# A tenth projection unit in seven products, thinner filler and an earlier softmax scaling in a neighbourhood attention layer

## The chip, the core and the metric

The kernel runs on one core of one Trainium2 chip. The metric is the device time of one execution in microseconds. The core's engines are TensorE (PE in the profile, PEld its weight loads), VectorE (DVE), ScalarE (ACT), GpSimd (POOL) and SyncE (SP), which here issues nearly all DMAs. Each runs its own instructions in the order of the program and waits for the others by semaphores.

## What is computed

One layer (DEPTH is 1) on 2048 tokens of width 1024, in float32, 16 heads of 64; the tokens form a grid of 32 rows of 64.

```
h = rmsnorm(x, norm_0)
q, k, v, gate = split(h @ w_in_0, 4)          # 1024 -> 4 x 1024
s = q . k / 8 + rpb                           # keys: 8 rows x 16 columns around the query
o = softmax(s) . v
x = x + (o * silu(gate)) @ w_out_0
out = rmsnorm(x, norm_f)
```

## The kernel before

Every product of the projections is made of three TensorE products in a faster 32-bit format: the operands are split into a high and a low part (ScalarE copies the high part, VectorE subtracts it), and high x high, high x low and low x high are summed.

Stage one and stage two make the projections of the first and of the second half of the tokens. A unit is 256 columns of q, k or gate (four units each, j = 0 to 3). "By seven" is Strassen's way: seven products of half the size on sums of the operands, 7 x 12 = 84 TensorE products of 128x512 for a unit and a token half, where the plain way takes 96. Stage two does nine units by seven (`units_two`); the last unit of q, k and gate (j = 3) is left for the attention loop, as `halves`: one entry is a unit on one quarter of the tokens, two `group`s of 24 products. `items` are the loads and splits that those need: weights ("w"), the last four blocks of x ("x", normalised on VectorE, split on ScalarE, remainder on VectorE) and the output weights ("o"). `consume` splits one item.

The attention loop (`for m in range(cycles + 1)`) runs over 32 cycles, one for each pair of heads and quarter of the tokens. This text calls round m the piece that begins with the transposes of cycle m - 1:

- `turns(m - 1)`: 44 transposes (`ph`) of the softmax weights; six copies to SBUF (`pta`), three on ScalarE (L1347), three on VectorE (L1345);
- `scores(2m)`, `scores(2m + 1)`: two runs of scores (`s`), each with four minima and sums on VectorE (L1306) and four exponentials on ScalarE (L1312);
- `values(m - 1)`: the product with v (`o`), its gating on VectorE (`og`, L1380) and its store (`ogd`);
- then, from the head of cycle m + 1, filler: products of `halves` (L392, L394, L396), later of the output projection (L1580, L1582, L1584). `feed(n)` issues about n of them; `amount` is the table of products for each cycle. Among them stands `normalise(2m + 1)`, the second run's softmax scaling: one reciprocal (L1317) and two products on VectorE (L1322), one on ScalarE (L1324), one on POOL (L1326). `consume` and `split_rows` stand there too.

What ends a group follows its last product: `give` for q, k and gate (gate: ScalarE's tanh L372, VectorE's `sg` L373), `add_rows` for output rows (`y`, L1452, later a Square, L1455). A clock counts the filler products, and `store` puts an action at a count: `load_q` and `load_k` of the next cycle stand at the counts 7 and 12 of a cycle, the store of `og` at 4 after `values`. What of the loads has not come by the end of a cycle is issued by `all_loads` at the next one's head. The first scaling, `normalise(2m)`, is issued within the second run of scores.

After the loop the last 12 of 16 row tiles of the output projection, six pairs, are made by seven as well (`rows_by_seven`).

Of the kernel before, what the change touches and what calls it, by code (L numbers as in the profile page):

```python
# [77 lines left out]
def build(ctx, tc, x, xr, xt, wg, bias, w_out, n0, nf, out):  # L78
# [178 lines left out]
    def units(k, j):  # L257
        return [KINDS[k] + j + i for i in range(2 if k == "v" else 1)]

    units_two = [(k, j) for j in range(3) for k in "kqg"]  # L260
    halves = [(k, 3, 1, c) for g in ("k", "qg") for c in (2, 3) for k in g]
    attending = [False]
    last_use = {}
    for n, (k, j, ph, c) in enumerate(halves):
# [5 lines left out]
    for n, (k, j, ph, c) in enumerate(halves):  # L270
        a = (KINDS[k] + j, ph)
# [36 lines left out]
    def consume(n, asked=False, turn=False):  # L308
        for _ in range(n):
            load_ahead()  # L310
            if attending[0] and not asked and not turn:
                return
            if state["used"] == len(items) or not may_use(items[state["used"]]):
                return
            if attending[0] and now() - asked_at[items[state["used"]]] < 36 and not asked:
                return
            it = items[state["used"]]
            state["used"] += 1
            use_item(it)
# [18 lines left out]
    def store(key, lag, f):  # L338
        n = len(later)
        while n and later[n - 1][0] > clock[0] + lag:  # L340
            n -= 1
        later.insert(n, (clock[0] + lag, key, f))

    def due(n):
        clock[0] += n
        while later and later[0][0] <= clock[0]:
            later.pop(0)[2]()
# [848 lines left out]
    def projections():  # L1196
        for n, (kind, j, ph, c) in enumerate(halves):
            state["half"] = n
            w = (KINDS[kind] + j, ph)
            for a in range(2):  # L1200
                if n == len(halves) - 5 and a == 0:
                    for k in range(RES_EARLY):
                        load_res(*turns_[k])
                if n == len(halves) - 1:
                    if a == 0:
                        load_og(0)
                        load_og(1)
                    else:
                        store(("og0",), 9, lambda: split_og(0))
                consume(1)  # L1210
                p = yield from group(w, a, c, n)
                state["event"] = clock[0]
                give(kind, 2 * j + a, c, p, True)
            state["done_halves"] = n + 1
# [191 lines left out]
    def load_og(n):  # L1406
        T, i = divmod(n, 4)
        must(*[("og", p, T) for p in range(NP)])
        G[n] = t = wp([128, NK, 128], F32, "ograw")
        nc.sync.dma_start(t, ogd[T][:, i])  # L1410

    def load_res(n, j):
        RES[n, j] = rbp([128, 512], F32, "xr")
        nc.sync.dma_start(RES[n, j], x[n * 128:n * 128 + 128, 512 * j:512 * j + 512])

    def split_og(n):
        t = G[n]
        state["event"] = clock[0]
        h, l = wp([128, NK, 128], F32R, "gh"), wp([128, NK, 128], F32R, "gl")
        for j in range(2):  # L1420
            s = slice(4 * j, 4 * j + 4)
            nc.scalar.activation(h[:, s], t[:, s], AF.Copy)
            nc.vector.tensor_tensor(l[:, s], t[:, s], h[:, s].bitcast(F32), OP.subtract)
        G[n] = [(h[:, i], l[:, i]) for i in range(NK)]
# [93 lines left out]
    def run_scales():  # L1518
        while rooted:
            n, scale, send = rooted.pop(0)  # L1520
            scale()
            store(("y", n), 18, send)
# [12 lines left out]
    def split_rows():  # L1535
        n = ready["split"]
        if rows_due():
            split_og(n)
            ready["split"] += 1
            return True  # L1540
# [201 lines left out]
                        f(*a)  # L1742

    cycles = len(order)
    dense, end_of_it = 13.5, 24
    amount = [dense] * 25
    first = 16
    amount[0] -= first / 2
# [1 line left out]
    for m in range(8, 24):  # L1750
        amount[m] += 1.5 if m % 2 == 0 else -1.5
    calm_debt = 3
    amount += [(96 * (12 - len(units_two)) + 48 * PLAIN - sum(amount) - first - end_of_it) / (cycles - 25)] * (cycles - 25) + [end_of_it]
    fill = projections()
    outs = outputs()
    credit = [0.0]
    alive = [True]

    def feed(n, calm=0):
        credit[0] += n  # L1760
        while credit[0] > 0 or credit[0] > -calm_debt and clock[0] - state["event"] < calm:
            if alive[0]:
                got = next(fill, None)
                if got is None:
                    alive[0] = False
                    continue
            else:
                got = next(outs, None)
                if got is None:
                    due(max(credit[0], 0.0))  # L1770
                    credit[0] = min(credit[0], 0.0)
                    return
            credit[0] -= got
            due(got)
# [30 lines left out]
    for m in range(cycles + 1):  # L1805
        a = amount[m] - 8
        begin(m)
        feed(8)
        if m:
            due_here = []  # L1810
            quiet[0] = True
            if a < 12 and m > 8 and m % 2:
                normalise(2 * m - 1, True, lambda: due_here.append(split_rows() or consume(1, turn=True)))
            else:
                normalise(2 * m - 1, True)
            most, behind = 99 if a > 12 else 0 if rows_due() else 1, bool(rooted)
            run_scales()
            if not (behind or any(due_here)):
                run_roots(most)
            for k in range(3):  # L1820
                if m == 1 and k == 2:
                    pass
                elif a > 12 or not any(due_here) and (k < 1 or k < 2 and m > 8 and m % 2 == 0):
                    got = split_rows()
                    due_here.append(got)
                    if not got:
                        consume(1, turn=True)
                    elif a < 12 and m % 2 == 0 and len(items) - state["used"] == 8:
                        feed(a * 0.2)
                        consume(1, turn=True)  # L1830
                feed(a * 0.2)
        else:
            feed(a * 0.6)
        quiet[0] = False
        feed(a * 0.4, 8 if a > 12 else 4)
        if m:
            turns(m - 1)
        if m == cycles:
            all_loads()
            feed(6)  # L1840
            while next(outs, 0) != 0:
                due(1)
            land_T2()
            for n in range(3):
                form_rows(n, 1)
        else:
            scores(2 * m)
            if m == 0:
                feed(first)
            scores(2 * m + 1, lambda: normalise(2 * m))  # L1850
            if m == 0:
                consume(2, turn=True)
        if m:
            values(m - 1)
        runs[0] += 1
        if m == 8:
            late_loads()
# [37 lines left out]
```

## Time and profile before

| | |
|---|---|
| median of 3 runs | 997.88 us (997.6 to 998.34) |
| profiled execution | 998.06 us, its span 996.0 us |
| TensorE busy | 986.9 us, 99% of the span, 6892 matmul records |
| VectorE, ScalarE, POOL busy | 772.9, 541.6, 128.5 us |
| granted TensorE clock | 0.999 |
| HBM | 160.31 MB read, 66.06 MB written, 227 GB/s |

The attention loop's first transposes begin at 575.3 us, its last at 871.4. A row of the timeline or of the chain begins with its start and its length in us, then the engine; `x44` counts the instructions that a row merges; what stands in brackets is idle time ahead of it and who ended it. A matmul's own length overlaps with the next one's, so the pace of TensorE is read from start to start. The rows that the prediction rests on stand there.

### The profile page before, as it was taken

The numbers are of one execution on the slowest core, as the hardware profiler recorded it, in microseconds if no ns is written. First come the engines' busy times: TensorE is split into PE (matmuls) and PEld (weight loads), VectorE is DVE, ScalarE is ACT, GpSimd is POOL, SyncE is SP. The second block draws the span as 40 slices with busy tenths as digits, with TensorE's granted clock in tenths as the row PEclk, the third lists the DMA queues.
The fourth block names the chain that finished last, engine by engine and source line by source line (L and its number), as shares of the span: only waits on it lengthen the run. The fifth ranks groups of instructions, "written<-read, shape, count | busy, mean of one in ns | idle before, by whom it ended". The sixth has DMA issues, their size and how long they took to land.

```text
span 996.0 us, 19496 instructions
## 1 busy us (share of the span) xinstructions
PE 986.9 (99%) x6892; PEld 789.4 (79%) x6892; DVE 772.9 (78%) x1703; ACT 541.6 (54%) x1310; POOL 128.5 (13%) x204
## 2 busy tenths in 40 slices
PE   9999999999999999999999999999999999999997
PEld 6888888888888888888888777777776777788886
DVE  5899888987665876766776687788889888886866
ACT  7863245465535442333433377777777786653443
POOL 0000001231100000000000022223232322201110
PEclk9999999999999999999999999999999999999999
DMA  8933547777947846656565798888978787997754
GB/s 285 347 116 104 195 134 255 246 250 251 363 150 222 275 123 194 205 174 213 175 191 195 229 286 270 271 240 261 320 231 290 244 251 236 329 358 199 196 153 116
DMA packets 150120, 227.65 MB, mean 229 GB/s; under 512 B 13640, under 2 KB 65096, under 8 KB 150024
## 3 DMA queue, kind: packets, MB, share of 16 engines
q1 hardware_dynamic: 147000, 221.30, 69.1%
q0 software_dynamic: 2592, 4.72, 2.9%
q8 instruction: 54, 0.88, 0.4%
q10 hardware_dynamic: 432, 0.40, 0.1%
q14 instruction: 42, 0.34, 0.1%
HBM read 160.31 MB, written 66.06 MB: 227 GB/s over the span
## 4 chain that ended last, share of the span: by engine, by line
PE 97%; ACT 1%; DVE 1%; DMA 0%; SPq 0%; issue 0%; POOL 0%; DVEq 0%; POOLq 0%
PE pp L448 40%; PE pv L614 13%; PE py L1674 11%; PE o L1376 8%; PE s L1297 7%; PE ph L1357 4%; PE pp L394 3%; PE pp L396 2%; PE pp L392 2%; PE pv L729 2%; PE po L1582 1%; PE po L1584 1%; PE po L1580 1%; DMA land<-in_xt_dram 0%; ACT x L1312 0%; DVE pta L1345 0%
## 5 line engine op out<-in xcount | busy, mean ns | idle before, releaser
L448 PE MATMUL pp<-h,f 128*128 128x512 f32 x576 | 185.4, 389 | 0.0
L448 PE MATMUL pp<-t,f 128*128 128x512 f32 x702 | 171.3, 389 | 0.0
L448 PEld LDWEIGHTS pp<-t,f 128*128 128x128 f32 x702 | 131.8, 188 | 27.4
L1326 POOL TENSOR_SCALAR x<-x,st 128x360 f32<-128x360 f32 (+5 forms) x160 | 81.8, 527 | 526.2 <-DVE st L1317 526.2
L1312 ACT ACTIVATE x<-x,st 128x360 f32<-128x360 f32 (+5 forms) x256 | 134.2, 526 | 26.9 <-DVE st L1306 26.8
L448 PEld LDWEIGHTS pp<-h,f 128*128 128x128 f32 x576 | 108.1, 188 | 22.5
L448 PE MATMUL pp<-l,f 128*128 128x512 f32 x288 | 112.1, 389 | 0.0
L1306 DVE CUSTOM_DVE_ANT_0 x<-s,em 128x360 f32<-128x360 f32 (+5 forms) x256 | 102.7, 457 | 2.2 <-issue 0.7
L431 DVE TENSOR_TENSOR f<-raw,f 128x512 fp32r<-128x512 f32 x105 | 75.8, 726 | 19.9 <-ACT f L430 19.7
L1376 PEld LDWEIGHTS o<-pta,vt 120*64 120x64 f32 (+2 forms) x1024 | 68.7, 137 | 22.4 <-DVE st L1306 15.2
L430 ACT ACTIVATE f<-raw 128x512 fp32r<-128x512 f32 x105 | 63.6, 622 | 37.1 <-DVE raw L437 22.0
L1376 PE MATMUL o<-pta,vt 120*64 120x192 f32 (+5 forms) x1024 | 83.5, 316 | 0.0
L1297 PE MATMUL s<-kt,q 64*64 64x360 f32 (+5 forms) x1024 | 73.1, 413 | 0.4 <-DVE pta L1345 0.3
L1347 ACT ACTIVATE pta<-ph 120x512 f32<-120x512 f32 (+5 forms) x96 | 48.9, 556 | 33.8 <-PE ph L1357 33.7
L1345 DVE COPY pta<-ph 120x512 f32<-120x512 f32 (+5 forms) x96 | 56.0, 638 | 13.4 <-PE ph L1357 13.1
L448 PEld LDWEIGHTS pp<-l,f 128*128 128x128 f32 x288 | 54.0, 188 | 11.3
L1674 PE MATMUL py<-woh,f 128*128 128x512 f32 x192 | 60.9, 390 | 0.0
L614 PE MATMUL pv<-wh,t 128*128 128x512 f32 x176 | 56.2, 389 | 0.0
L1297 PEld LDWEIGHTS s<-kt,q 64*64 64x64 f32 x1024 | 36.5, 132 | 21.7 <-DVE pta L1345 4.9
L448 PE MATMUL pp<-sixths,f 128*128 128x512 f32 x198 | 52.7, 389 | 0.0
L1357 PEld LDWEIGHTS ph<-ident,x 64*120 64x120 f32 (+2 forms) x1408 | 42.6, 128 | 11.7 <-issue 10.6
L430 ACT ACTIVATE f<-s 128x512 fp32r<-128x512 f32 x42 | 26.2, 624 | 45.6 <-DVE s L437 40.4
(227 smaller groups left out, 1872.8 us busy)
## 6 DMA issues: line engine op xcount, KB each, us to landing
raw<-in_wg_dram SPq DMA_DIRECT2D x124, 256.0 KB, 5.1
row<-in_xr_dram SPq DMA_DIRECT2D x32, 256.0 KB, 5.4
vd<-v SPq DMA_DIRECT2D x32, 256.0 KB, 5.0
sgd<-sg SPq DMA_DIRECT2D x32, 256.0 KB, 3.2
q<-qd SPq DMA_DIRECT2D x32, 256.0 KB, 5.8
sgt<-sgd SPq DMA_DIRECT2D x32, 256.0 KB, 7.0
ogd<-og SPq DMA_DIRECT2D x32, 256.0 KB, 3.4
kt<-kd SPq DMA_DIRECT2D x16, 480.0 KB, 6.4
```

The costliest lines, as they stand in the source:

```text
L430: nc.scalar.activation(t[:, 0], src, AF.Copy)
L431: nc.vector.tensor_tensor(t[:, 1], src, t[:, 0].bitcast(F32), OP.subtract)
L448: nc.tensor.matmul(B[n, P], t[:, int(m == 2), c], x[k][int(m == 1)], start=P in (1, 6, 5) and k == 0 and m == 0, stop=k == 3 and m == 2, s ...
L614: nc.tensor.matmul(p, a[:, o], b, start=P in (1, 6, 5) and k == 0 and m == 0, stop=k == 3 and m == 2, skip_group_check=True)
L1297: nc.tensor.matmul(places[C, s][h * 64:h * 64 + 64], qt[a, g * 64:g * 64 + 64], kt[a, :r1 - r0, c0:c0 + 8 * WIDE[C]].rearrange("p r (s c) ...
L1306: nc.vector.tensor_tensor_reduce(X[i, C][s], pst[s], EM[p, ROW_TYPE[T]][C > 0][s], -1.0, 1e38, OP.add, OP.min, st[:, o:o + 1])
L1312: nc.scalar.activation(X[i, C][s], X[i, C][s], AF.Exp, bias=st[:, o:o + 1], scale=-1.0, accum_out=st[:, 4 + o:5 + o])
L1326: nc.gpsimd.tensor_scalar(X[i, C][s], X[i, C][s], st[:, o:o + 1], 1.0, op0=OP.mult, op1=OP.mult)
L1345: nc.vector.tensor_copy(o, i_)
L1357: nc.tensor.transpose(ph[b, h][:k, o:o + 64], X[2 * m + late_, group[g]][s][q, at:at + k], ident[q, q])
L1376: nc.tensor.matmul(o[s * 64:s * 64 + 64, g0 * 64:g1 * 64], vt[:k, strip, s * 64:s * 64 + 64], t[:k, n * 64:(n + g1 - g0) * 64], start=stri ...
L1674: nc.tensor.matmul(B[m, P], t[:, a, c], b, start=P in (1, 6, 5) and k == 0 and i == 0, stop=k == 3 and i == 2, skip_group_check=True)
```

## The change

The k unit j = 3 joins `units_two`, so stage two does ten units by seven and the loop is left with q and gate of j = 3, in four halves. `dense`, the base of `amount` for the first 25 cycles, goes from 13.5 to 10.8; the later ones take what is left. The head of a cycle issues 5 (`HEAD`) instead of 8 filler products before `normalise`, and the other 3 after the first split. The hooks that load residual rows, the first rows of the output projection and split them are set to the halves that are left, and that split comes at the count 14 instead of 9.

```
-    units_two = [(k, j) for j in range(3) for k in "kqg"]
-    halves = [(k, 3, 1, c) for g in ("k", "qg") for c in (2, 3) for k in g]
+    units_two = [(k, j) for j in range(3) for k in "kqg"] + [("k", 3)]
+    halves = [(k, 3, 1, c) for c in (2, 3) for k in "qg"]
...
-                if n == len(halves) - 5 and a == 0:
+                if n == 0 and a == 1:
                     for k in range(RES_EARLY):
                         load_res(*turns_[k])
                 if n == len(halves) - 1:
-                    if a == 0:
+                    if a == 1:
                         load_og(0)
                         load_og(1)
-                    else:
-                        store(("og0",), 9, lambda: split_og(0))
+                        store(("og0",), 14, lambda: split_og(0))
...
-    dense, end_of_it = 13.5, 24
+    dense, end_of_it = 10.8, 24
...
+    HEAD = 5
...
-        feed(8)
+        feed(HEAD)
...
-                feed(a * 0.2)
+                feed(a * 0.2 + (8 - HEAD if k == 0 else 0))
         else:
-            feed(a * 0.6)
+            feed(a * 0.6 + 8 - HEAD)
```

Counted in the order of TensorE's instructions, the filler products of rounds 1 to 31 were 11 14 13 14 13 14 15 | 12 15 12 15 12 15 15 12 12 15 12 15 12 18 9 15 | 12 13 14 13 14 13 17 20, and are 11 11 11 10 11 11 13 | 9 15 6 12 10 12 9 13 10 12 12 9 9 12 10 11 | 9 12 7 9 10 9 13 20 (the bars stand behind rounds 7 and 23). In the changed kernel the line numbers of the places below are one lower.

VectorE in round 0, from behind the minima and sums to the copies of round 1, before (`raw` and `l` are a block of x, its normalised form and its low part; `w` a weight's low part; `x` the softmax weights, `pta` their transposes):

```order
L542 SCALAR_TENSOR_TENSOR raw<-raw,g_174,rb 128x512
L547 TENSOR_TENSOR l<-raw,h 128x512
L542 SCALAR_TENSOR_TENSOR raw<-raw,g_174,rb 128x512
L547 TENSOR_TENSOR l<-raw,h 128x512
L1317 RECIPROCAL st<-st 128x4
L1322 TENSOR_SCALAR x_5286<-x_5286,st 128x264
L1322 TENSOR_SCALAR x_5287<-x_5287,st 128x264
L194 TENSOR_TENSOR w<-raw,w 128x512 x2
L1345 COPY pta<-ph_5374 88x6x64
```

And in the changed kernel, at the same place:

```order
L194 TENSOR_TENSOR w<-raw,w 128x512 x2
L1316 RECIPROCAL st<-st 128x4
L1321 TENSOR_SCALAR x_5423<-x_5423,st 128x264
L1321 TENSOR_SCALAR x_5424<-x_5424,st 128x264
L542 SCALAR_TENSOR_TENSOR raw<-raw,g_174,rb 128x512
L547 TENSOR_TENSOR l<-raw,h 128x512
L542 SCALAR_TENSOR_TENSOR raw<-raw,g_174,rb 128x512
L547 TENSOR_TENSOR l<-raw,h 128x512
L1344 COPY pta<-ph_5503 88x6x64
```

The two blocks of x have changed places with the two weights, and stand between the scaling and the copies; two more blocks, not shown, stand at the same place in rounds 1 and 2, where one weight stood.

VectorE in round 14, from the gating to the copies of round 15, before (`wol` is the low part of an output weight):

```order
L1380 TENSOR_TENSOR og<-o,sgt 128x512
L1317 RECIPROCAL st<-st 128x4
L1322 TENSOR_SCALAR x_7679<-x_7679,st 128x360
L1322 TENSOR_SCALAR x_7680<-x_7680,st 128x360
L199 TENSOR_TENSOR wol<-raw,woh 128x512 x2
L1345 COPY pta<-ph_7760 120x6x64
```

And in the changed kernel (`sg` is the gate's evacuation, which waits for its group of products and for ScalarE's tanh):

```order
L1379 TENSOR_TENSOR og<-o,sgt 128x512
L373 SCALAR_TENSOR_TENSOR sg<-sg,pp 128x512
L1316 RECIPROCAL st<-st 128x4
L1321 TENSOR_SCALAR x_7773<-x_7773,st 128x360
L1321 TENSOR_SCALAR x_7774<-x_7774,st 128x360
L199 TENSOR_TENSOR wol<-raw,woh 128x512 x2
L1344 COPY pta<-ph_7845 120x6x64
```

The gate's evacuation now stands ahead of the reciprocal, and the two splits are still there; it stands so in rounds 3 and 12 too (before: in 11 and 18).

SyncE's queue around the loads of q and keys (`kt`) for round 12, before (`ogd` is the store of `og`, `vt` the values, `kd_69` the keys of the third pair of heads):

```order
L1383 DMA ogd_87<-og 512x1x128
L1254 DMA vt<-vd_83 120x1024
L1268 DMA em<-in_bias_dram 128x360
L374 DMA sgd_81<-sg 128x512
L1268 DMA em<-in_bias_dram 128x480
L1245 DMA q<-qd_61 128x512
L1236 DMA kt<-kd_69 128x960
L1259 DMA sgt<-sgd_76 128x512
L1383 DMA ogd_86<-og 512x1x128
```

And in the changed kernel:

```order
L1382 DMA ogd_87<-og 512x1x128
L1253 DMA vt<-vd_83 120x1024
L1267 DMA em<-in_bias_dram 128x360
L1267 DMA em<-in_bias_dram 128x480
L1244 DMA q<-qd_61 128x512
L381 DMA qd_66<-q 128x512
L1382 DMA ogd_86<-og 512x1x128
L1235 DMA kt<-kd_69 128x960
L1258 DMA sgt<-sgd_76 128x512
```

The keys of round 12 have gone behind the next store of `og`, that of the values made in round 11; the keys of round 28 stand behind the store made in round 27 in the same way.

## The prediction

> **What bounds the kernel now.** I read the page first (its chain), then the chain in order of time, then the timelines of VectorE and SyncE inside single rounds of the attention loop.
>
> ```profile
> PE 97%; ACT 1%; DVE 1%; DMA 0%; SPq 0%; issue 0%; POOL 0%; DVEq 0%; POOLq 0%
> PEclk9999999999999999999999999999999999999999
> ```
> ```profile
> 389.35 171.36 PE pp L448 x756
> ...
> 575.35 1.36 PE ph L1357 x44
> ...
> 601.76 1.36 PE ph L1357 x44
> ...
> 610.87 1.36 PE ph L1357 x44
> ...
> 657.41 1.44 PE ph L1357 x44
> ...
> 666.71 1.44 PE ph L1357 x44
> ...
> 670.53 2.54 PE o L1376 x32
> ...
> 676.69 1.44 PE ph L1357 x44
> ...
> 823.41 1.36 PE ph L1357 x44
> ...
> 832.46 1.36 PE ph L1357 x44
> ...
> 841.74 1.36 PE ph L1357 x44
> ...
> 871.40 1.36 PE ph L1357 x44
> ```
>
> TensorE is the bound: 97% of the chain, at full clock. One 512-column product costs 171.36 / 756 = 0.2267 us. In the attention loop a round runs from the transposes (ph) to the next ph: ph, scores, values, then filler products, whose number I count in the order of the instructions. The rounds from 601.76, 666.71 and 823.41 have 14, 15 and 13 of them, so without fillers a round takes 9.11 - 3.17 = 5.94 us (rounds 1 to 7), 9.98 - 3.40 = 6.58 (8 to 23) and 9.05 - 2.95 = 6.10 (24 to 31). Values begin 3.82 after ph in the middle kind (666.71 to 670.53). From 575.35 to 871.40 lie 31 rounds, 296.05 us; by those bases they need 7 x 5.94 + 15 x 6.58 + 7 x 6.10, 12.7 for the two of mixed kind, and 426 products of 0.2267: 292.2 together. So only **3.8 us** of the loop is TensorE waiting.
>
> **VectorE's own round** is nearly as long. From one round's copies (L1345) to the end of its second scaling (L1322), in the three kinds of round:
>
> ```profile
> 593.48 1.74 DVE L1345 COPY pta<-ph 88x384 f32<-88x384 f32 x3
> ...
> 599.86 0.86 DVE L1322 TENSOR_SCALAR x<-x,st 128x264 f32<-128x264 f32 x2
> ```
> ```profile
> 657.98 1.76 DVE L1345 COPY pta<-ph 120x384 f32<-120x384 f32 x3 [0.80 <-PE ph L1357]
> ...
> 664.88 1.04 DVE L1322 TENSOR_SCALAR x<-x,st 128x360 f32<-128x360 f32 x2
> ```
> ```profile
> 832.31 1.40 DVE L1494 SCALAR_TENSOR_TENSOR y<-y,st,acc 128x512 f32<-128x512 f32 x2
> 833.63 1.74 DVE L1345 COPY pta<-ph 96x384 f32<-96x384 f32 x3
> ...
> 840.03 0.91 DVE L1322 TENSOR_SCALAR x<-x,st 128x288 f32<-128x288 f32 x2
> 840.86 0.20 DVE L1479 TENSOR_SCALAR st<-st 128x1 f32<-128x1 f32 x1
> ...
> 842.44 1.74 DVE L1345 COPY pta<-ph 96x384 f32<-96x384 f32 x3
> ```
>
> That is 7.24, 7.94 and 7.31 us; the next instruction starts 0.08 before such an end (832.31 + 1.40 is 833.71, the copies start at 833.63), so 7.16, 7.86 and 7.23. Extras that stand between scaling and copies come on top: the final norm's eight small operations 1.58 (840.86 to 842.44), two final scalings 1.32 (832.31 to 833.63), any other 512-wide operation about 0.61. When this round is longer than TensorE's, the copies come late and, past a margin, TensorE waits. Two places show what that costs:
>
> ```profile
> 777.00 1.44 PE ph L1357 x44
> ...
> 785.88 1.29 DVE wol L199 x2
> ...
> 790.04 2.54 PE o L1376 x32
> ```
> ```profile
> 784.47 1.04 DVE L1322 TENSOR_SCALAR x<-x,st 128x360 f32<-128x360 f32 x2
> ...
> 787.09 1.75 DVE L1345 COPY pta<-ph 120x384 f32<-120x384 f32 x3
> ```
>
> This round has 9 products: 6.58 + 2.04 = 8.62. Values should begin at 777.00 + 8.62 + 3.82 = 789.44 and begin at 790.04: **0.60 us lost**. The copies came at 787.09; by the 0.57 between ph and copies (657.98 against ph at 657.41) they should at 786.19: 0.90 late. So in the middle rounds 0.3 of a lateness is free and is carried on, the rest is TensorE's. In the last rounds the copies at 833.63 were 0.60 late and the next ph still came on time (9.28 for 14 products): there I take 0.8 as the free part; the first rounds, built alike, get the same. Two splits (L199) cost 787.09 - 785.52 + 0.08 = 1.65 here, 785.52 being the scaling's end, with a Square ahead on ScalarE; without that I estimate 1.37.
>
> ```profile
> 735.69 1.44 PE ph L1357 x44
> ...
> 744.07 0.69 DVE sg L373
> ...
> 745.04 0.69 POOL x L1326
> 745.78 1.21 PE ph L1357 x33
> ...
> 750.25 2.54 PE o L1376 x32
> ```
>
> Here, with 12 products, the gate's sg (L373) is queued ahead of the second reciprocal, so the scaling on POOL ends late: ph ends at 746.99 and not at 744.99 + 1.44, **0.56 lost**, and values begin another 0.88 late. Half of all the waiting of today stands in these two readings.
>
> **Part by part.** *The tenth unit by seven.* 96 fillers leave the loop (21.76 us), 84 products join stage two (19.04): **-2.72 us**. Stage two has cover for the unit's forms and sums:
>
> ```profile
> 525.00:550.00 25.00, 25.00 (x112) 20.71 (x111) 14.55 (x23) 10.04 (x19) 0.00 (x0) 1.00 0.54 179
> ```
>
> VectorE is busy 14.55 of 25 there and TensorE never pauses: nothing added. If a load failed that cover, one landing of some 6 us would be the price; I see no reason.
>
> *Filler 10.8.* Rounds 1 to 31 hold 338 products instead of 426, and VectorE's work does not shrink with them. *First rounds.* An x item (normalise, split on ScalarE, remainder on VectorE, one after the other) takes 573.33 - 571.22 = 2.11:
>
> ```profile
> 571.22 0.75 DVE L542 SCALAR_TENSOR_TENSOR raw<-raw,g,rb 128x512 f32<-128x512 f32 x1
> ...
> 573.33 0.17 DVE L1317 RECIPROCAL st<-st 128x4 f32<-128x4 f32 x1
> ```
>
> Today two items stand ahead of the reciprocal of round 0, while VectorE waits for the exponentials anyway. Now two stand behind it and one more behind the scaling of rounds 1 and 2. In round 0, in today's times, the reciprocal would come at some 571.9 and not 573.33, its scaling end at 572.9, the items at 577.1; the copies are wanted at 575.35 + 0.57 less 5 products of 0.2267, 574.8: 2.3 late, 1.5 lost. Rounds 1 and 2 (11 products, 5.94 + 2.49 = 8.43): 0.8 carried + 7.16 + 2.11 - 8.43 = 1.6 late, 0.8 lost each. Behind round 3, late by the 0.8, sg stands ahead of the scaling: another 0.9. **First rounds: 4.0.**
>
> *Middle rounds*, TensorE's round (base, products) against 7.86 and the extras:
> - 8 (9 products, two splits, base 6.5): 9.23 against 8.55: 0.4 lost.
> - 10 (6 products, two splits): 9.23 against 7.94: 1.0, some of it because the scaling ends after ph begins.
> - 12 (10 products, sg ahead): the reading of 0.56, plus 0.45 for two products less, less 0.68 since the group ends at the second filler and not the fifth: 0.3 to 0.4.
> - 14 (9 products, sg ahead, two splits): 0.56 + 0.68 - 0.23, and 0.85 for the splits: 1.9.
> - 16 (10 products, two gl, one y): 9.84 against 8.85: 0.7. 17 and 18 (12 products): 0.2 and 0.5. 19 (9 products, two splits behind a Square, 0.3 carried): the reading of 0.60 plus 0.3: 0.9.
>
> **Middle: 6.0**, nearly all after rows of today's profile.
>
> *Last rounds*, 7 to 13 products: 24, 25, 27, 28, 29 and 30 each carry 1.3 to 1.9 of extras on 7.23 (8.8 to 9.2) against 8.1 to 9.05. After the free 0.8 is used up, 0.3 + 0.7 + 0.3 + 0.1 + 0.3 + 0.7 + 0.1, and 0.6 behind round 26 (7 products, a Square ahead of the scaling on ScalarE): **3.1**.
>
> *Keys.* A key load is stored up for the 12th filler product; where a round has 6 or 7, it is issued at the next round's start, behind the store of og. That happens twice, for rounds 12 and 28:
>
> ```profile
> 673.84 0.52 SPq L1383 DMA_DIRECT2D ogd<-og  x1
> 674.47 1.28 SPq L1254 DMA_DIRECT2D vt<-vd  x1
> ```
> ```profile
> DMA to landing us min/median/max: 6.2/6.7/7.2
> ```
>
> The store waits for og, 673.84 - 666.71 = 7.1 after ph, and the queue's next issue follows 0.63 later. Keys issued there in round 11 land, at the 6.2 of the shortest row (today's stand behind three or four other loads, so I take no more), 14.0 after its ph; the scores of round 12 want them at 6.58 + 2.72 + 1.44 = 10.7. **3.3 lost**. In SyncE's program kt stands first behind the store, so the other end is a landing in 3 us: 0.1. For round 28 the same sum is about 13.5 against 9.5: 4.0, other end 0.8. All products stand behind those scores in TensorE's program. I take 3.3 + 3.9 = **7.2**, by the rows of the same load, and 1 to 9 as bounds. The page's clock row shows full speed through every pause of up to about 1 us; it has no pause of 3 or 4 us, so the sum keeps full speed.
>
> [...]
>
> *Earlier issue of the scaling (fifth filler).* What moves is the reciprocal, two products on VectorE, one on ScalarE, one on POOL, past evacuations alone, and no DMA. It gains only where an evacuation came with products 6 to 8; at products 2 and 4 it still stands ahead (rounds 3, 12, 14). *Residual rows, first og loads and their split at 14:* loads off every path, with a round of cover or more: 0; without it, one landing.
>
> Sum: -2.7 + 4.0 + 6.0 + 3.1 + 7.2 - 3.8 (today's waits, which these replace) = +13.8. The profiled execution took 998.06 (span 996.0), 0.2 over the median of 997.88; the forecast against the median is **1011.7 us**.
>
> **Rivals.**
> 1. *Faster*: the round is TensorE's after all. If the order took the scalings out from behind sg and VectorE's round then fitted (it decides at 7.86 + extras under 6.58 + 0.2267 x products), the 2.0 us of the two readings go and 2.7 with them: 993.1. For it: 3.8 us of waiting today. Against it: a 9-product round with two splits has already lost 0.60. Chance 0.05; with half of the terms gone and nothing left either way, 0.03 for no change.
> 2. *Keys in time*: they land in about 3 us, since they stand first in the queue: 1011.7 - 6.3 = 1005.4. For it: only 0.5 MB precede; against it: no landing of kt under 6.2. Chance 0.15.
> 3. [...] Chance 0.05.
>
> Forecast 0.72. **Range:** low end: keys at 1 and the first rounds at 1.5 (their free part might be larger, no row of today tests it) gives 1003; high end: keys 9, first rounds 6: 1016. What a measurement can tell from no change is 0.2%, 2 us: faster 0.05, same 0.03, slower 0.92.
>
> **What would show it.** In the new profile: chain rows of VectorE copies, L199, L542 or POOL x between ph and scores in rounds 1 to 4, 9, 11, 13, 15, 17 to 20 and in the last ones; scores of rounds 12 and 28 released by kt, 3 us late; stage two unbroken; TensorE's busy time shorter by 2.7. Wrong it would be if the chain stays on TensorE in the short rounds, so that late copies cost nothing, or if kt landed before the transposes end.

## The result: 1.4% slower, and where the time went

The changed kernel takes 1011.39 us (median of four runs, 1009.67 to 1014.78), the kernel before 997.74 beside it (996.92 to 998.34): a ratio of 1.0138, 95% interval 1.0117 to 1.0159. The forecast was 1011.7. The profiled execution of the changed kernel took 1009.67, 11.6 more than that of before (998.06).

Most line numbers of the loop are one lower after the change (scores L1296, transposes L1356, copies L1344, scalings L1321 and L1325). From the page of the changed kernel, whose span is 1007.9 us (996.0 before), the chain that ended last:

```profile
PE 92%; DMA 2%; ACT 2%; DVE 2%; issue 1%; SPq 0%; POOL 0%; DVEq 0%; POOLq 0%
```

TensorE had 97% of the chain before; of the five points that it lost, two lie with the keys' DMA and one each with ScalarE, VectorE and "issue", time in which the engine waited for nothing that the profile shows. The timeline of TensorE gives the bounds of stage two and of the loop: the first product of stage two, then the loop's first and last transposes, of after and then of before:

```profile
388.46 0.39 PE L448 MATMUL pp<-h,f 128*128 128x512 f32 x1
...
591.78 0.42 PE L1356 MATMUL ph<-ident,x 64*88 64x64 f32 x8
...
883.25 0.93 PE L1356 MATMUL ph<-ident,x 64*96 64x64 f32 x26
```
```profile
389.19 0.39 PE L448 MATMUL pp<-h,f 128*128 128x512 f32 x1
...
575.28 0.93 PE L1357 MATMUL ph<-ident,x 64*88 64x64 f32 x26
...
871.33 0.87 PE L1357 MATMUL ph<-ident,x 64*96 64x64 f32 x24
```

From the start of stage two to the loop's first transposes pass 203.3 us where 186.1 passed. The 17.2 us more are the price of 76 products at the prediction's 0.2267 (84 more in stage two, 8 fewer in round 0), so nothing waits there. Stage two itself began 0.7 earlier in this execution; over all kernels run here its start lies between 388.2 and 389.2, so I take this for scatter. The loop takes 291.5 us where it took 296.0. By the prediction's bases (195.7) and 338 products (76.6) it needs 272.3, so **19.2 us of waiting** stand where 3.8 stood. 17.2 - 0.7 - 4.6 makes 11.9, the difference of the spans. TensorE's waits in the loop, as the view of waits groups them (us in total, times, longest):

```profile
PE s L1296 <- DMA kt<-kd: 5.0, 2, 2.9
PE ph L1356 <- POOL x L1325: 1.4, 3, 0.7
PE s L1296 <- DVE y L1451: 0.8, 2, 0.5
PE s L1296 <- ACT pta L1346: 0.7, 1, 0.7
PE s L1296 <- DVE pta L1344: 0.3, 1, 0.3
```

The view shows 8.2 of the 19.2. The rest stands inside pieces of work: scores whose weight loads wait for a copy come out as a longer row, in round 11 (682.92 to 686.03) 3.1 us in place of 2.4. I therefore took each piece of a round (transposes, scores, values, fillers) from the start of its first instruction to that of the next piece's first, and subtracted the length that it has in an undisturbed round (transposes 1.36 or 1.44, scores 1.79, 2.38 or 1.94).

**The keys of round 12.** SyncE's timeline, then TensorE's in rounds 12 and 28:

```profile
689.40 0.53 SPq L1382 DMA_DIRECT2D ogd<-og  x1
689.99 0.62 SPq L1235 DMA_DIRECT2D kt<-kd  x1
```
```profile
695.15 4.14 PE L1296 MATMUL s<-kt,q 64*64 64x240 f32 x32 [2.13 <-DMA kt<-kd]
...
847.22 2.01 PE L1296 MATMUL s<-kt,q 64*64 64x192 f32 x32 [2.88 <-DMA kt<-kd]
```

The load stands behind the store of og and lands 5.2 us after its issue (689.99 to 695.15). The waits are 2.1 and 2.9 us. But the scores of round 12 then take 4.14 us where an undisturbed row of this view has 2.45. The view by windows shows why; its columns are the stretch, its length, busy time of PE, PEld, DVE, ACT, POOL, then the granted clock, the DMA share and GB/s:

```profile
692.32:695.73 3.41, 1.28 (x36) 1.13 (x36) 1.58 (x3) 1.34 (x3) 0.00 (x0) 1.00 0.91 245
695.73:699.14 3.41, 3.41 (x28) 1.34 (x19) 2.64 (x11) 2.61 (x9) 0.00 (x0) 0.50 1.04 301
...
842.50:845.90 3.40, 1.84 (x47) 1.34 (x45) 3.16 (x12) 1.63 (x4) 0.31 (x1) 1.00 1.08 318
845.90:849.30 3.40, 2.08 (x34) 1.42 (x36) 1.23 (x6) 0.51 (x3) 0.00 (x0) 1.00 0.96 242
```

For 3.41 us behind the wait (695.73 to 699.14) the granted clock is 0.50; that costs 1.7 us, the 4.14 less 2.45 of these scores. Around the longer wait of round 28 it is 1.00. So of the 19.2 us the keys make 6.8, the first rounds 3.4, the middle ones (9 to 20) 5.9 and the last ones (24 to 31) 3.2, which together fit to 0.1. (In round 24 the undisturbed scores are the 1.94 of the kernel before; counted against 2.38, the last rounds come to the 2.8 that the expectations below name.)

**The first rounds**, VectorE and TensorE around round 1:

```profile
590.43 0.73 DVE L542 SCALAR_TENSOR_TENSOR raw<-raw,g,rb 128x512 f32<-128x512 f32 x1
...
593.91 0.69 DVE L547 TENSOR_TENSOR l<-raw,h 128x512 fp32r<-128x512 f32 x1 [0.70 <-ACT h L546]
594.52 1.74 DVE L1344 COPY pta<-ph 88x384 f32<-88x384 f32 x3
```
```profile
593.14 0.52 PE L1296 MATMUL s<-kt,q 64*64 64x176 f32 x4
594.30 2.09 PE L1296 MATMUL s<-kt,q 64*64 64x176 f32 x28 [0.65 <-ACT pta L1346]
```

Two x items hold VectorE from 590.43 to 594.52, and the scores of round 1 take 3.19 from 593.14 on, not 1.79.

**The middle**, VectorE and TensorE at the head of round 15:

```profile
722.12 0.69 DVE L373 SCALAR_TENSOR_TENSOR sg<-sg,pp 128x512 f32<-128x512 f32 x1 [1.06 <-ACT sg L372]
722.72 0.17 DVE L1316 RECIPROCAL st<-st 128x4 f32<-128x4 f32 x1
...
724.14 1.29 DVE L199 TENSOR_TENSOR wol<-raw,woh 128x512 fp32r<-128x512 f32 x2 [0.17 <-ACT woh L198]
725.35 1.75 DVE L1344 COPY pta<-ph 120x384 f32<-120x384 f32 x3
```
```profile
723.82 1.22 PE L1356 MATMUL ph<-ident,x 64*120 64x64 f32 x33 [0.74 <-POOL x L1325]
724.97 3.32 PE L1296 MATMUL s<-kt,q 64*64 64x240 f32 x32
```

The gate's sg stands ahead of the second reciprocal, two splits behind the scaling: the transposes lose 1.0 and the scores 0.9.

### The profile page after: what moved, and what is told of

It is laid out like the page before. It is cut to its first block, busy times and chain, and to the rows that moved or that the text cites. A ratio compares the mean times of both kernels' runs of the same rounds, so it can differ in the third digit from the quotient of the medians.

```text
span 1007.9 us, 19489 instructions
## 1 busy us (share of the span) xinstructions
PE 992.2 (98%) x6880; PEld 789.3 (78%) x6880; DVE 779.9 (77%) x1715; ACT 542.7 (54%) x1311; POOL 126.7 (13%) x204
## 4 chain that ended last, share of the span: by engine, by line
PE 92%; DMA 2%; ACT 2%; DVE 2%; issue 1%; SPq 0%; POOL 0%; DVEq 0%; POOLq 0%
PE pp L448 41%; PE pv L614 13%; PE py L1673 11%; PE o L1375 7%; PE s L1296 7%; PE ph L1356 4%; PE pv L729 2%; ACT x L1311 2%; DMA kt<-kd 2%; PE po L1581 1%; PE po L1583 1%; PE po L1579 1%; PE pp L394 1%; PE pp L396 1%; PE pp L392 1%
## 5 line engine op out<-in xcount | busy, mean ns | idle before, releaser
L448 PE MATMUL pp<-h,f 128*128 128x512 f32 x608 | 195.7, 389 | 0.0
L448 PE MATMUL pp<-t,f 128*128 128x512 f32 x728 | 178.0, 389 | 0.0
L448 PEld LDWEIGHTS pp<-t,f 128*128 128x128 f32 x728 | 136.6, 188 | 28.4
L1325 POOL TENSOR_SCALAR x<-x,st 128x360 f32<-128x360 f32 (+5 forms) x160 | 80.9, 521 | 540.1 <-DVE st L1316 529.3
L448 PEld LDWEIGHTS pp<-h,f 128*128 128x128 f32 x608 | 114.1, 188 | 23.8
L448 PE MATMUL pp<-l,f 128*128 128x512 f32 x304 | 118.3, 389 | 0.0
L431 DVE TENSOR_TENSOR f<-raw,f 128x512 fp32r<-128x512 f32 x110 | 79.3, 725 | 19.5 <-ACT f L430 19.4
L430 ACT ACTIVATE f<-raw 128x512 fp32r<-128x512 f32 x110 | 66.5, 622 | 39.2 <-DVE raw L437 22.2
L1296 PE MATMUL s<-kt,q 64*64 64x360 f32 (+5 forms) x1024 | 79.5, 424 | 6.9 <-DMA kt<-kd 5.0
L448 PEld LDWEIGHTS pp<-l,f 128*128 128x128 f32 x304 | 57.1, 188 | 11.9
L1296 PEld LDWEIGHTS s<-kt,q 64*64 64x64 f32 x1024 | 37.3, 133 | 33.5 <-DVE pta L1344 11.8
L1344 DVE COPY pta<-ph 120x512 f32<-120x512 f32 (+5 forms) x96 | 55.9, 637 | 6.1 <-PE ph L1356 6.0
L448 PE MATMUL pp<-sixths,f 128*128 128x512 f32 x208 | 55.6, 389 | 0.0
L1356 PEld LDWEIGHTS ph<-ident,x 64*120 64x120 f32 (+2 forms) x1408 | 43.3, 128 | 13.6 <-issue 8.5
```

The costliest lines, as they stand in the source:

```text
L430: nc.scalar.activation(t[:, 0], src, AF.Copy)
L431: nc.vector.tensor_tensor(t[:, 1], src, t[:, 0].bitcast(F32), OP.subtract)
L448: nc.tensor.matmul(B[n, P], t[:, int(m == 2), c], x[k][int(m == 1)], start=P in (1, 6, 5) and k == 0 and m == 0, stop=k == 3 and m == 2, s ...
L1296: nc.tensor.matmul(places[C, s][h * 64:h * 64 + 64], qt[a, g * 64:g * 64 + 64], kt[a, :r1 - r0, c0:c0 + 8 * WIDE[C]].rearrange("p r (s c) ...
L1325: nc.gpsimd.tensor_scalar(X[i, C][s], X[i, C][s], st[:, o:o + 1], 1.0, op0=OP.mult, op1=OP.mult)
L1344: nc.vector.tensor_copy(o, i_)
```

## Experiments

All times are medians, beside runs of the kernel before on the same chip; ratios are to that. The three lines that experiment 4 adds shift the line numbers of experiments 4, 6, 7, 9 and 12 (scores L1299).

**1. Keys ahead of the store.** An edit of the changed kernel:

```
-            later_loads([load_q(*nx), load_k(*nx)], 7, 5)
+            later_loads([load_q(*nx), load_k(*nx)], 5, 0.9)
```

> The changed kernel, with one thing undone: the loads of the next queries and keys no longer fall due at the 7th and 12th filler product but at the 5th and just behind it, so that in rounds 11 and 27 too SyncE issues the keys ahead of the store of og, as in all other rounds. Nothing else moves. Theory (order in the queue): the scores of rounds 12 and 28 find their keys, and the two waits of 2.1 and 3.0 us go, and with them the stretch at half clock behind the first (1.7 us): 6.9 us less than the profiled execution of the changed kernel, 1002.8 us, granted clock back at .999, and the runs' spread of 5 us shrinks to under 2 us. Rival (the load itself is slow, or the DMA engines are full there): the scores still wait for kt by 2 us or more, 1008 to 1012 us.

Measured: 1004.28 us (1003.40 to 1005.48), ratio 1.0057 (1.0046 to 1.0069). SyncE and TensorE, the same keys and scores:

```profile
682.55 0.43 SPq L1235 DMA_DIRECT2D kt<-kd  x1
```
```profile
692.88 2.45 PE L1296 MATMUL s<-kt,q 64*64 64x240 f32 x32
```

The keys go out 7.4 us earlier, the scores wait for nothing and run at full clock (1.00 from 691.44 to 702.00). The profiled execution is 6.3 shorter (1003.40; 6.9 expected), the spread of the runs 2.1 us in place of 5.1. The edit makes the loads of queries and keys fall due earlier in every round, but it changes nothing else, and nothing waited for keys in the other rounds; so the place of these two loads behind the store is shown as the cause of the two waits. For the spread it is the likely cause: the kernels with executions at a granted clock of .997 or less (the changed kernel down to .995) are those whose trace has a wait for keys of 2 us or more. One execution of the kernel before is the exception (.996, 1003.16 us); its profiled execution has no such wait, and why that one was slow is not known.

**2. The second scaling at the eighth product again.** The changed kernel with:

```
-    HEAD = 5
+    HEAD = 8
```

> The changed kernel, with the second scaling of a run issued at the eighth filler product again, as before the change (six pairs, ten units and filler 10.8 stay). In the order of the program the fillers are spread more evenly then (rounds 8 to 11 have 11, 13, 9, 9 instead of 9, 15, 6, 12), so the keys of round 12 are issued ahead of the store; those of round 28 are not. Theory (the queue and VectorE's round count, the earlier scaling hardly): the wait of round 12 with its half-clock stretch goes (3.8 us), rounds 9 and 10 lose less (about 0.5), the gate's sg stands ahead of a reciprocal in one round more (0.4 lost): 3 to 5 us less, some 1005.7 us. Rival (the earlier scaling brings what it costs in order, 2 us or more): no faster than the changed kernel, 1010 us or more.

Measured: 1009.13 us, ratio 1.0104 (1.0090 to 1.0118), an interval that just touches the changed kernel's; profiled execution 1008.12, only 1.6 less. Its loop is 2.5 us shorter (289.0 for 291.5), but stage two began 0.7 later. The wait of round 12 and its slow stretch are gone, 3.8 us, but round 28, which kept its wait (2.44 us), now got the half clock: 0.50 in the second row below, 1.6 us, the 3.65 of its scores less 2.01. The waits that are not for keys come to 12.2 us, against 12.3: what the more even filler saves in rounds 9 to 11 (1.4) is lost at other places, 0.9 at the transposes of round 6 alone, where sg stands ahead of the reciprocal and I had allowed 0.4. So both theories were off. In the changed kernel the earlier scaling shows no net gain: what it saves behind sg, 1 to 2 us by this reading, it gives back by the order of the fillers, and it puts the keys of round 12 behind the store. The stretch ahead of the slow one of round 28 and the slow one, by windows (columns as above):

```profile
841.05:844.46 3.41, 1.02 (x33) 0.87 (x31) 2.95 (x5) 1.46 (x3) 0.00 (x0) 1.00 1.06 207
844.46:847.87 3.41, 3.36 (x32) 1.98 (x32) 1.36 (x9) 0.96 (x5) 0.00 (x0) 0.50 0.97 236
```

**3. The earlier scaling alone.** The kernel before with the changed kernel's `HEAD = 5` and the three `feed` calls that use it:

```
-        feed(8)
+        feed(HEAD)
...
-                feed(a * 0.2)
+                feed(a * 0.2 + (8 - HEAD if k == 0 else 0))
...
-            feed(a * 0.6)
+            feed(a * 0.6 + 8 - HEAD)
```

> The kernel before, with the earlier scaling alone (fifth filler product; five pairs... and nine units by seven, filler 13.5 stay). Theory: the gate's sg no longer stands ahead of the second reciprocal in rounds 11 and 18, so the readings of 0.9 to 1.4 us in each go; the splits that move behind sg find rounds with 15 and 16 products and cost 0.2 to 0.5: 1.3 us less (0.8 to 2.2), 996.4 us. Rival (issuing it earlier costs, since products 6 to 8 lose their cover): 1 us more than before, 998.7 us.

Measured: 995.37 us, ratio 0.9965 (0.9951 to 0.9979): 3.4 us faster, more than twice the 1.3 that I expected and outside the range given. VectorE behind round 18 (in the prediction's row the sg at 744.07 stood ahead of the reciprocal), and TensorE's only wait in the loop that the view lists:

```profile
742.05 0.18 DVE L1317 RECIPROCAL st<-st 128x4 f32<-128x4 f32 x1 [0.17 <-ACT x L1312]
742.27 1.04 DVE L1322 TENSOR_SCALAR x<-x,st 128x360 f32<-128x360 f32 x2
743.38 0.69 DVE L373 SCALAR_TENSOR_TENSOR sg<-sg,pp 128x512 f32<-128x512 f32 x1
```
```profile
PE s L1297 <- DMA kt<-kd: 0.4, 1, 0.4
```

Of the 3.8 us of waiting 0.9 stay. Besides the 2.5 at the two places with sg, 0.6 went in round 21 and 0.2 in round 23; the wait for keys is new.

**4. The x items ahead of the weights of g.** The changed kernel with three more lines behind the list of items:

```
+    xs_ = [i for i in items if i[0] == "x"]
+    ws_ = [i for i in items if i[0] == "w"]
+    items = ws_[:4] + xs_ + ws_[4:]
```

> The changed kernel, with the four x items loaded and made ahead of the weights of g, not behind them (their order alone): two of them stand ahead of the second reciprocal of round 0, where VectorE waited anyway, and rounds 1 and 2 carry a weight's remainder of 0.65 us in place of an x item of 2.1 us. Theory (VectorE's round sets the first rounds): of the 3.4 us that rounds 0 to 4 lost in the profiled execution 1.0 to 1.5 stay, 1007.7 us (1.5 to 2.7 us less), the waits for keys unchanged at 2 to 3 us each. Rival (the first rounds wait for something else, the loads of the round or the ph banks): the scores of rounds 1 to 3 still begin 0.6 to 1.4 us late, 1009.5 us or more.

Measured: 1009.61 us, ratio 1.0109 (1.0092 to 1.0125). By this median the theory's 1007.7 was missed, and the interval overlaps the changed kernel's, so the times alone show no gain; the four executions that were not profiled had a granted clock of .996 or .997. The trace tells the two theories apart. In the profiled execution (1006.60, clock .999) the scores of round 1 take 2.62, those of rounds 2 and 3 their undisturbed 1.79, the transposes of round 4 1.78: 1.3 us stay of the 3.4, as the theory has it, so VectorE's round set the first rounds. The two key waits (2.2 and 3.1 us) stay; no half clock came behind them in this execution (the scores take their undisturbed 2.45 and 2.01), which by itself makes it 1.7 us shorter.

**5. Splits on POOL.** The changed kernel, in the output weights' split and, in the same way, in that of og:

```
-            nc.vector.tensor_tensor(l, t, h.bitcast(F32), OP.subtract)
+            nc.gpsimd.tensor_tensor(l, t, h.bitcast(F32), OP.subtract)
```

> The changed kernel, with one kind of work taken off VectorE: the remainders of the output weights' and of og's split (wol and gl, 512 wide) are computed on POOL, which is idle for 5 to 6 us of every round; nothing else moves. Theory (VectorE's round sets the middle rounds): 0.6 to 0.7 us less on VectorE for each, so that of the 5.9 us lost in rounds 8 to 20 the parts behind rounds 8, 10, 16, 17, 18 and 19 go (0.4, 1.0, 0.7, 0.2, 0.5, 0.9) and of the 1.9 behind round 14 some 0.5; those behind sg stay: 4 us less than the profiled execution, 1005.7 us, the waits for keys unchanged. Rival (the losses come with the number of fillers alone, or from ScalarE's squares and splits): no change, 1009 to 1011 us. Third: POOL, slower by itself, is late with its scalings: over 1012 us.

Measured: 1006.26 us, ratio 1.0075 (1.0062 to 1.0088), clearly under the changed kernel's 1.0138. POOL in round 18, and the scores of round 19:

```profile
759.32 2.54 POOL L199 TENSOR_TENSOR wol<-raw,woh 128x512 fp32r<-128x512 f32 x2 [0.36 <-ACT woh L198]
```
```profile
761.31 2.45 PE L1296 MATMUL s<-kt,q 64*64 64x240 f32 x32
```

A split takes 1.27 us on POOL, twice the 0.65 on VectorE (1.29 for the two of round 14), but POOL stood idle for 6.8 us there in the changed kernel (761.70 to 768.52). All losses behind rounds 8 and 16 to 19 are gone, that behind round 10 has fallen from 1.0 to 0.3; what stays behind sg is 0.3 and 1.0, about as expected: 1.6 us of the 5.9 in all. So VectorE's round set the middle rounds. This execution took 1009.66 although its middle rounds lost 4.3 us less, since its keys of round 28 came later (a wait of 4.7 us); behind the second wait the clock was 0.50 for 6.83 us (841.68 to 848.51). Behind the first I estimate one such stretch of 3.41, from the mean granted clock: .994 over the span of 1007.4 us is 6.0 us lost, of which those 6.83 make 3.4 and the kernel's end 0.8, if it is as in the changed kernel (0.50 for the last 1.55 us):

```profile
691.50:694.91 3.41, 1.46 (x45) 1.31 (x44) 1.76 (x3) 1.56 (x3) 0.00 (x0) 1.00 0.93 236
838.27:841.68 3.41, 1.43 (x45) 1.28 (x44) 3.06 (x12) 1.52 (x3) 0.00 (x0) 1.00 1.00 295
841.68:845.10 3.42, 0.69 (x9) 0.64 (x13) 0.00 (x0) 0.00 (x0) 0.00 (x0) 0.50 0.92 242
```

**6. All mends.** Edits 1, 4 and 5 together, and `HEAD = 1`, which puts every sg behind the scaling.

> The changed kernel with the four mends together: keys ahead of the store of og, x items ahead of the weights of g, wol and gl on POOL, and a run's second scaling issued at the first filler product (so that sg is behind it in every round). If the parts add: 1009.67 less 6.3 for the keys, 2.5 for x, 4.0 for POOL and 1.5 to 2 for sg, 995.5 us; what is left are the last rounds (2.8 us, with 8 to 12 products each) and 1 to 1.5 of others. Rival: losses only move on (what is carried from round to round comes out later): 999 us or more.

Measured: 995.28 us (994.98 to 995.60), ratio 0.9968 (0.9956 to 0.9980). The parts add: the expected sum was 995.5 (its terms give 994.9 to 995.4). It means that the losses of the changed kernel were in the main separate waits, each with its own cause, and not one that moves from place to place. Two reservations: the part for sg was not run by itself in the changed kernel, and the last rounds now lose 3.7 us for 3.2, so a little does move.

**7. Mends and filler 10.0.**

```
-    dense, end_of_it = 10.8, 24
+    dense, end_of_it = 10.0, 24
```

> The kernel of the four mends with filler 10.0 in place of 10.8: rounds 4 to 22 have some 0.8 products less each, the last seven 11 to 13 and not 8 to 12. Theory: VectorE's round (7.23 and 1.3 to 1.9 of extras) then fits under TensorE's in the last rounds (6.10 and 0.2267 for each product: 8.6 to 9.05), and they lose under 0.7 in place of 2.8; the middle rounds, without splits on VectorE, pass at 8 or 9 products or lose some tenths. 993.5 us, 2 us under the one with 10.8. Rival: the middle rounds give back what the last ones gain: no difference, 995.5 us.

Measured: 997.03 us, ratio 0.9986 (0.9978 to 0.9995). Slower than with 10.8, but not for the rival's reason: the chain of waits goes back through the keys of round 10 to SyncE, where a load stood for 5.9 us in the view of SyncE's waits.

```profile
662.59 2.02 SPq L1247
664.66 6.16 DMA kt<-kd
```
```profile
SPq L171 <- POOL wol L199: 7.7, 3, 5.9
```

L171 loads the raw output weights five items ahead into six buffers, so it waits for the split just queued on POOL, and the keys wait behind it. The keys of round 25, 1.2 us late, were issued behind a load of a residual row that had waited 6.8 us for a Square on ScalarE.

**8. The kernel before with the same treatment** (edit 5 and `HEAD = 1`).

> The kernel before (nine units by seven, filler 13.5), with the second scaling issued at the first filler product and wol and gl on POOL. It lost 3.8 us in its loop, and with the scaling at the fifth product alone its trace shows 1.0 left. Theory: nearly nothing waits any more, 994.0 us (0.4 to 1.2 less than with the earlier scaling alone), and it can go no lower, since its loop and its stage two are TensorE's. If the tenth unit by seven is worth its 2.7 us, the mended changed kernel should pass under it; if not (rival: that unit costs as much elsewhere), this one stays the fastest.

Measured: 1000.87 us, ratio 1.0032 (1.0020 to 1.0044), slower than before; the expectation fell. Waits of SyncE and of TensorE:

```profile
SPq L171 <- POOL wol L199: 7.3, 2, 6.6
```
```profile
PE s L1297 <- DMA kt<-kd: 4.0, 3, 2.1
```

The same mechanism: the load that waits 6.6 us for POOL, and that nobody needs yet, stands ahead of the keys of round 14 (2.1 us of TensorE's). The keys of round 24 (1.8 us) were issued late too, behind a load of a residual row that had waited 8.1 us for ScalarE. The kernel before has such a wait of 7.8 us as well and no wait for keys, so for round 24 that load alone does not explain it.

**9. Two loads out of SyncE's way**, on top of experiment 7:

```
-    AHEAD = 5
+    AHEAD = 4
...
-        nc.sync.dma_start(RES[n, j], x[...
+        nc.scalar.dma_start(RES[n, j], x[...
```

> The kernel of the four mends with filler 10.0, with two loads taken out of SyncE's way: the raw weights are loaded one item later (four ahead, not five, so that no load waits on SyncE for the buffer whose remainder POOL still reads), and the residual rows are loaded from ScalarE's queue, where the square that frees their buffer stands just ahead. Theory (the filler-10 version lost its gain to keys queued behind a load that waited for its buffer, 5.9 us on POOL and 6.8 us on ScalarE): its waits of 1.6 and 1.2 us for keys go, 997.35 less 2.8 to 3.4, 994.2 us. Rival (the keys are late by the DMA engines, or ScalarE pays for the issues): 996.5 us or more.

Measured: 995.38 us, ratio 0.9967 (0.9954 to 0.9979), profiled execution 994.44. TensorE waits for keys nowhere any more, so the queue is shown as the cause in 7, though not how much each of the two loads had cost. 3.7 us are left, half of them in rounds 26 and 28, where the chain runs from the final scaling and y on VectorE through a Square and the load's issue on ScalarE to the copies:

```profile
827.51 1.32 DVE y L1496 x2
828.83 0.61 DVE y L1454
...
830.00 0.20 ACT xr L1457
...
830.22 0.34 ACTq L1416
...
830.60 0.50 ACT pta L1349
...
831.14 0.94 PE s L1299 x9
```

**10. The same two loads in the kernel of experiment 8.**

> The kernel before with the second scaling at the first filler product, wol and gl on POOL, and the same two loads out of SyncE's way. Theory: the two waits for keys of 2.1 and 1.9 us behind the load that waited 6.6 us for POOL go: 999.96 less 4.0, 996 us; what stays are 0.8 us each at the norm's operations in two of the last rounds. Rival: as without, 1000 us or more.

Measured: 997.51 us, ratio 0.9992 (0.9983 to 1.0001): 3.4 less than experiment 8. The two waits of experiment 8 are gone, but a new one of 0.9 us stands in round 16. So 996 was missed, and by its interval this kernel cannot be told from the kernel before.

**11. The same with `HEAD = 5`.**

> The same with the second scaling at the fifth filler product (where the norm's operations stand as in the kernel with the earlier scaling alone). Theory: that kernel's 994.85 less its last waits of 0.5 and 0.4 us: 994.0 us. Rival (POOL's work or ScalarE's issues cost as much): 995 us or more.

Measured: 997.02 us (995.49 to 1000.74), ratio 0.9987 (0.9973 to 1.0001). Missed, and not to be told from the kernel before either: I had taken the half microsecond that experiment 3 loses in round 16 for VectorE's. It was its one wait for keys. SyncE and TensorE here:

```profile
707.86 1.06 SPq L1410 DMA_DIRECT2D ograw<-ogd  x2
709.17 0.60 SPq L1236 DMA_DIRECT2D kt<-kd  x1
```
```profile
718.80 3.60 PE L1297 MATMUL s<-kt,q 64*64 64x240 f32 x28 [2.26 <-DMA kt<-kd]
```

Two loads of og, 512 KB each, stand just ahead of the keys here, in experiment 3 and in experiment 10. Here the keys land 9.6 us after their issue (709.17 to 718.80). Why they land later here than in experiment 3, where the wait was 0.4, or experiment 10, where it was 0.9, was not settled. The profiled execution (999.73) is the second longest of eleven; it also loses 1.0 us in round 18, where the transposes wait for a scaling on POOL, and 0.6 in round 1. The half clock came behind this wait too, 0.50 in the second row, with the stretch before it in the first:

```profile
714.97:718.38 3.41, 1.57 (x45) 1.37 (x44) 1.76 (x3) 1.56 (x3) 0.78 (x1) 1.00 1.11 360
718.38:721.79 3.41, 2.99 (x24) 1.71 (x28) 1.34 (x7) 1.09 (x5) 0.00 (x0) 0.50 0.99 307
```

**12. Filler 10.4** with all edits of experiment 9.

> The kernel of the four mends and the two loads out of SyncE's way, with filler 10.4 in place of 10.0: rounds 24 to 29 have 11 products each, the middle ones 6 to 14, and the norms stand otherwise among the rounds. With filler 10.0 the profiled execution lost 3.7 us in its loop, 1.8 of it in rounds 26 and 28, where a square, a split of og and a load's issue on ScalarE stand ahead of the copies. Theory (those meet only where the norm's operations, a y and a split fall into one round): 1 to 2 us lost in all, 992 to 993.5 us. Rival (ScalarE's round is as full as VectorE's, so what is taken out of one round comes out in another): 994.5 us or more, as with 10.0 and 10.8.

Measured: 994.59 us (993.91 to 994.82), ratio 0.9965 (0.9951 to 0.9979), profiled execution 994.82. The rival's figure: rounds 26 and 28 lose nothing any more, but rounds 27 and 29 lose 1.25 and 0.5 and others some tenths each, 3.7 us in all as before. Whether ScalarE is what fills these rounds, as the rival has it, was not tested. It is no faster, by these intervals, than experiments 3, 6 and 9. Four versions thus end at 0.9965 to 0.9968, all of them faster than both kernels, and the simplest is the kernel before with the earlier scaling alone. That the tenth unit by seven gains anything once its waits are mended was not shown: from the start of stage two to the loop's last transposes experiment 12 takes 479.1 us and experiment 3 479.2, so the 2.7 us of products that the unit saves came back as waiting (3.7 us for 0.9).

## Why the prediction was right, point by point

- **TensorE's sum.** -2.7 for twelve products fewer came as forecast: stage two and round 0 take 17.2 more without any wait, the loop's work without waits 20.0 less by the prediction's bases. One sign named for it failed: TensorE's busy time did not fall by 2.7 but rose, 986.9 to 992.2, since rows with a wait inside (3.17 us in round 11) and the stretch at half clock (busy 3.41 of 3.41) count as busy. The records of matmuls fell by twelve, 6892 to 6880.
- **VectorE's round.** This carried 13.1 of the sum and held: 3.4 in the first rounds for 4.0, 5.9 for 6.0, 3.2 for 3.1. In the middle the eight named places each came to within 0.1. In the last rounds the total is partly luck: 0.6 of it stands behind round 23, for which the sum had no term, and the named places gave 2.7. Experiments 4 and 5 took away the named work in the first and the middle rounds, and most of the named losses went; the last rounds were not taken apart in this way. The sum of 4.0 was too large by 0.1 to 0.2 for each of its four places.
- **Keys.** The mechanism was right and experiment 1 shows it; two sizes were off against each other. The landing, taken as 6.2 from loads with others ahead of them, was 5.2, and 5.0 us of waits came for 7.2. But the sum kept full clock, and the half clock came behind one of the two waits (+1.7). Rival 2, a landing in about 3 us, fell.
- **The clock.** The sum kept full speed because the page had no pause of 3 or 4 us, and had no term for a lower clock. It was 0.50 behind some of the waits for keys (round 12 of the changed kernel, round 28 in experiments 2 and 5, round 16 in experiment 11) and not behind others (round 28 of the changed kernel, both of experiment 4). In the changed kernel full clock came back after 3.41 us, which makes the price 1.7 us; in experiment 2 it was 1.6.
- **The earlier scaling** was called free, with a gain only where an evacuation came with products 6 to 8. In the kernel before that is where it gained most: 3.4 us alone. In the sum those places are the larger part of the -3.8 of today's waits, and I called these "replaced" by the new ones. They did go, but by which part of the change is not shown: with the scaling at the eighth product the changed kernel does not have them at these places either (experiment 2), and the gain of 3.4 does not carry over to it.
- **The total.** The profiled execution shows +11.6 against +13.8. Its terms, 3.4 + 5.9 + 3.2 + 6.8 of new waits for a forecast of 20.3, missed by 1.0, mostly in the first rounds and the keys; another 0.7 is the earlier start of stage two. That the median met the forecast to 0.3 us is partly luck: other executions had a lower granted clock (.995 and .996 at 1014.78 and 1012.75), and no term stood for that.

## What to carry to other kernels

When filler is taken out of a loop that hides another engine's work, compare that engine's round with the new TensorE round, extras included, round by round: nearly each place where it was longer by more than a few tenths could be named ahead and priced from a row of the old profile, and in the middle rounds moving the extra to a free engine mended it (4.3 of 5.9 us in experiment 5). In a queue that carries critical loads, look for a store or a load that waits for its buffer ahead of them: the keys behind the store went out 7.4 us later than ahead of it (experiment 1), and those behind a load that waited 6.6 us cost TensorE 2.1 (experiment 8). Look too where a trigger by count falls past the end of a short round. Take an edit apart before judging it, and in both kernels: here one part gained 3.4 us by itself in the kernel before, and taking it out of the changed kernel made that no slower, so the gains of the parts did not add.

## What the runs showed of the hardware that I had not expected

The granted clock fell to 0.50 behind stretches in which TensorE had been partly busy. In the 3.41 us ahead of a halved stretch it was busy 1.28 us (changed kernel, round 12), 1.02 (experiment 2, round 28), 1.43 (experiment 5, round 28) and 1.57 (experiment 11, round 16), transposes included. In the changed kernel the wait of round 28 lies across 842.50 to 845.90 and 845.90 to 849.30; there it was busy 1.84 and 2.08 and the clock stayed at 1.00. These are busy times of the profile, which models the ends of matmuls.

The length of the wait alone does not tell the two apart: waits of 2.13 us (changed kernel, round 12), 2.26 (experiment 11) and 2.44 (experiment 2) were followed by 0.50, while behind 2.88 us (changed kernel, round 28) and 2.06 (experiment 8, round 14) the scores took their undisturbed 2.01 and 2.45. What decides between them was not shown.
